# Wider value and gate projections, and a later start for two gated heads, in the second block's mixers

## The chip, the cores and the metric

One core of a Trainium2 chip runs the whole program. The metric is device time in microseconds (us): one launch from its first to its last instruction and the little that lies around it. Lower is better.

## The reference, cut to what matters

The program computes two blocks of two layers each for 512 tokens of width 1024, in fp32. The change touches only the mixer of the second block, which runs in both of its layers on 512 latent tokens and on 256 context tokens:

```python
lat, cx = project_in(h, w_in), project_in(hc, w_in)     # h @ w_in, split in ten parts
# ret: q, k, v, gate (512 columns each)   gla: q, k (256 each), v, gate (512 each), two decay inputs (16 each)
r = bidirectional_scan(retention_inputs)     # 4 heads of 128; q and k of the latent are rotated
g = bidirectional_scan(gla_inputs)           # 4 gated heads: keys of 64, values of 128, decay per key
y = concat(head_layernorm(r) * silu(ret_gate), rmsnorm(g, gla_norm_g) * silu(gla_gate))
x = x + g1 * (y @ w_out)
```

The latent scans start from the final states of the context scans. Layer 0 needs the mixer's output for the context too; layer 1 needs only its states.

## The kernel before, in words

Every large matrix product is done in three passes of fp32r matmuls (`mat3`; matmuls are recorded at L169, transposes at L186): both operands are split in a high and a low part, and hi·hi, hi·lo and lo·hi are added in PSUM. A weight block is loaded by SyncE (`wload`, L258), its high part is cast on ScalarE (ACT, L262), its low part subtracted on VectorE (DVE, L263); three blocks are in flight.

`linear` has the weights stationary and streams the tokens, 512 columns at a time for the latent. `linear_tm` has 128 tokens stationary and streams the weights; with `cn` = 256 columns two token tiles share a PSUM bank (`per` = 2), with 512 each token tile has its own bank. It opens all its banks at the start, goes through the weight blocks, and copies the banks out behind the last one, with a raised priority. In a trace a matmul of `linear_tm` reads `whi,hi` or `wlo,hi` (weights first), one of `linear` `hi,whi`.

PSUM has four banks for these products: three called `mm` and one called `bank`, which every fourth call gets. Three more are `pt` (transposes and small products), one is `po` (outputs of the heads).

`hybrid` sets up one mixer. Its projections run in a fixed order. For the latent: the decay input, the gated keys (`twice`), the gated values (`values`), the gated queries, the gated heads' gates (`gates`), the retention's keys (`heads`, L1272, rotated on GpSimd and VectorE), the retention's values, its queries, its gates. `values` and `gates` call `linear_tm` twice, with 256 columns (two heads) each. In layer 0 the context does the same but for the order of one gate; in layer 1 it has neither queries nor gates.

The heads are Python generators beside that: four gated heads (`gla`) and four retention heads (`retention`), at most two of each kind at a time (`pipe`). A generator yields a condition to wait for or a delay in planned TensorE time, so the order in which instructions are emitted is fixed when the program is built. A tile scheduler then orders each engine's queue by priority (early emission first) and by when tiles are free; on the chip every engine follows its queue in order. Most working tiles come from one pool of 36 slots (`t2`); the values of layer 1's latent have another pool (`b2`).

A gated head first turns the decay input into decays (L1417 to L1430: three activations, a scan and five VectorE operations), multiplies keys and queries (L1435 to L1443), transposes, forms scores, updates states and ends in `finish`, which multiplies by the gate (L1330), transposes, and splits the result (L420; L417 for the retention) into `y`. `y` is filled in order: gated heads 0 to 3, retention heads 0 to 3. Last comes the output product `w_out`: first the half of the gated heads, then that of the retention. In layer 0 the context's output product runs before it.

Of the kernel before, what the change touches and what calls it, by code (L numbers as in the profile page):

```python
# [13 lines left out]
AF = mybir.ActivationFunctionType  # L14
ALU = mybir.AluOpType
# [3 lines left out]
D = 1024  # L19
# [32 lines left out]
def sl(i, n=128):  # L52
    return slice(i * n, (i + 1) * n)
# [28 lines left out]
class Net:  # L82
# [1138 lines left out]
    def hybrid(self, l, h, w, st_in, st_out, outputs, rot, y):  # L1221

        nc, A = self.nc, self.A
        W = A["w_in_2"][l]
# [3 lines left out]
        V, G, F = {}, {}, {}  # L1228

        vtile = self.b2 if st_out is None and l else self.t2  # L1230

        def values(key, c0):
            for s in range(2):
                def evac(q, p):
                    t = vtile(nm="v")
                    self.evicted = nc.scalar.copy(t, p.rearrange("p i c -> p (i c)")).ins
                    for ii in range(2):
                        for hh in range(2):
                            V[key, 2 * s + hh, 2 * q + ii] = t[:, sl(ii, 256)][:, sl(hh)]

                yield from self.linear_tm(W, 0, D, c0 + 256 * s, 256, h, w, evac)

        def gates(key, c0):
            for s in range(2):
                def evac(q, p):
                    u, t = self.t2(nm="gate_in"), self.t2(nm="gate")
                    self.evicted = nc.scalar.copy(u, p.rearrange("p i c -> p (i c)")).ins
                    nc.scalar.activation(t, u, AF.Abs)
                    nc.scalar.activation(t, t, AF.Exp, scale=-1.0)
                    nc.scalar.activation(t, t, AF.Ln, bias=self.one[:, 0:1])  # L1250
                    nc.vector.scalar_tensor_tensor(t, u, 0.0, t, ALU.min, ALU.subtract)
                    nc.scalar.activation(t, t, AF.Exp)
                    nc.gpsimd.tensor_mul(t, t, u)
                    for ii in range(2):
                        for hh in range(2):
                            G[key, 2 * s + hh, 2 * q + ii] = t[:, sl(ii, 256)][:, sl(hh)]

                yield from self.linear_tm(W, 0, D, c0 + 256 * s, 256, h, w, evac)

        def narrow(nm):  # L1260

# [147 lines left out]
            yield from finish("r", hd, po.rearrange("p i c -> p (i c)"), True)  # L1409

        def gla(hd):
            yield lambda: "d" in F and ("gk", hd) in F
            p = self.pt((128, w))
            self.mat(p, self.gup[:, hd], F["d"])
            ub = self.vec("gla_gate_b_2", l * 4 + hd)
            a, b, c = (self.t2(nm=s, w=w) for s in ("ga", "gb", "gc"))
# [30 lines left out]
            p = self.pt((128, w))  # L1447
# [26 lines left out]
            for _ in range(nch // 4):  # L1474
                t = self.t2(nm="S")
# [27 lines left out]
            for cix in range(nch):  # L1503
                i, j = divmod(cix, 2)
# [3 lines left out]
        def project():  # L1508
            yield from gate_in()
            yield from twice("gk", 2304, 1.0)  # L1510
            yield from values("g", 2560)
            if outputs:
                yield from twice("gq", 2048, 0.125)
                if st_out is None:
                    yield from gates("g", 3072)
            yield from heads("rk", 512, 1.0)
            yield from values("r", 1024)
            if outputs:
                yield from heads("rq", 0, 128 ** -0.5)
                if st_out is not None:  # L1520
                    yield from gates("g", 3072)
                yield from gates("r", 1536)

        return ([self.pipe(deque(Stream(f(i)) for i in range(4)), 2) for f in (gla, retention)], project())

    def second_layer(self, l):
# [246 lines left out]
```

## Time and profile before

| what | value |
|---|---|
| median of 3 runs | 3194.77 us (3189.08 to 3195.32) |
| the profiled execution | 3192.44 us |
| its span, first to last instruction | 3190.7 us |
| TensorE busy | 3115.1 us, 98% |
| VectorE / ScalarE / GpSimd busy | 57% / 38% / 7% |
| mean granted TensorE clock | 0.991 |
| latent mixer of layer 0 / layer 1 | about 1608 to 1840 us / 2520 to 2753 us of the span |

Busy TensorE time counts from the start of a matmul to its modelled end, and neighbouring matmuls overlap; what a matmul costs in a row of its like is the distance between starts. The granted clock is a share of full speed: 1.0 is 2.4 GHz, 0.5 is 1.2 GHz.

### The profile page before, as it was taken

The page shows a single profiled execution, that of the slowest core. Times are in us where ns is not written, and L with a number is a line of the kernel's source. Part 1 is how long each engine was busy: PE and PEld are TensorE (multiplying, and loading weights), DVE is VectorE, ACT ScalarE, POOL GpSimd, SP SyncE. Part 2 cuts the span into 40 slices and gives each one's busy share as a digit, 9 for nine tenths or more (in the row PEclk, how much of TensorE's full clock was granted, in tenths as well). Part 3 has the DMA queues.
Part 4 walks back from the last instruction along what each step waited for, and adds up shares of the span by engine and source line. Part 5 has one row for each costly group of instructions (what it writes and reads, how often), then busy time and mean ns, then how long its engine had stood idle before and what let it go on. Part 6 is the DMA issues. An engine that isn't in the chain of part 4 may idle for free.

```text
span 3190.7 us, 45206 instructions
## 1 busy us (share of the span) xinstructions
PE 3115.1 (98%) x17958; PEld 2651.7 (83%) x17958; DVE 1804.6 (57%) x3261; ACT 1221.0 (38%) x2189; POOL 214.3 (7%) x263
## 2 busy tenths in 40 slices
PE   8999999999999999999998999999999998999998
PEld 8866678888997888888987998888888887978887
DVE  7865474445566664445776675333334767764444
ACT  5734342223554542223554353132222544342233
POOL 0200000000111000000121230000000012200000
PEclk9999999999999999999999999999999999999999
DMA  5357843333321223333532232121211522223332
GB/s 153 113 190 266 269 131 98 99 93 110 89 82 56 86 85 94 99 98 95 152 101 72 83 100 65 61 67 60 67 60 52 151 74 73 77 77 99 94 98 73
DMA packets 301858, 323.99 MB, mean 102 GB/s; under 512 B 18832, under 2 KB 270608, under 8 KB 301648
## 3 DMA queue, kind: packets, MB, share of 16 engines
q1 hardware_dynamic: 296656, 315.22, 32.0%
q10 hardware_dynamic: 4992, 5.90, 0.6%
q8 instruction: 141, 2.31, 0.3%
q14 instruction: 69, 0.57, 0.1%
HBM read 310.05 MB, written 2.10 MB: 98 GB/s over the span
## 4 chain that ended last, share of the span: by engine, by line
PE 92%; DVE 4%; DMA 1%; issue 1%; ACT 1%; SPq 0%; POOL 0%; ACTq 0%; DVEq 0%; POOLq 0%
PE mm L169 63%; PE bank L169 17%; PE pt L169 5%; PE po L169 3%; PE pt L186 2%; PE bank L1058 2%; DMA raw<-in_w_mem_kv 1%; DVE wlo L263 0%; PE mm L186 0%; DVE ht L1094 0%; DVE gc L1422 0%; DVE sq L381 0%; ACT whi L262 0%; DMA dup<-dup 0%; DMA ada<-in_ada_w 0%
## 5 line engine op out<-in xcount | busy, mean ns | idle before, releaser
L263 DVE TENSOR_TENSOR wlo<-raw,whi 128x1024 fp32r<-128x1024 f32 (+1 forms) x503 | 594.3, 1183 | 681.0 <-ACT whi L262 667.3
L262 ACT CAST whi<-raw 128x1024 fp32r<-128x1024 f32 (+1 forms) x503 | 505.4, 1006 | 1227.0 <-PE mm L169 821.6
L169 PE MATMUL mm<-hi,whi 128*128 128x512 f32 (+2 forms) x2276 | 723.2, 355 | 7.1 <-ACT hi L1098 2.7
L169 PE MATMUL mm<-hi,wlo 128*128 128x512 f32 (+2 forms) x1876 | 688.7, 367 | 0.8 <-DVE wlo L263 0.8
L169 PE MATMUL mm<-lo,whi 128*128 128x512 f32 (+2 forms) x1476 | 575.7, 390 | 4.5 <-DVE lo L1099 4.2
L169 PEld LDWEIGHTS mm<-hi,whi 128*128 128x128 f32 (+1 forms) x2276 | 403.5, 189 | 79.1 <-issue 6.7
L169 PEld LDWEIGHTS mm<-hi,wlo 128*128 128x128 f32 (+1 forms) x1876 | 354.6, 189 | 64.4 <-issue 7.0
L169 PE MATMUL mm<-ahi,whi 128*128 128x512 f32 (+1 forms) x1224 | 392.1, 355 | 0.0
L169 PE MATMUL mm<-ahi,wlo 128*128 128x512 f32 (+1 forms) x1032 | 377.4, 368 | 0.0
L169 PEld LDWEIGHTS mm<-lo,whi 128*128 128x128 f32 (+1 forms) x1476 | 279.3, 189 | 63.3 <-DVE lo L1099 4.7
L169 PE MATMUL mm<-alo,whi 128*128 128x512 f32 (+1 forms) x840 | 323.4, 387 | 0.0
L169 PE MATMUL mm<-whi,hi 128*128 128x256 f32 (+2 forms) x1008 | 272.2, 292 | 18.7 <-ACT qk L1272 10.3
L169 PE MATMUL mm<-wlo,hi 128*128 128x256 f32 (+2 forms) x896 | 258.8, 290 | 0.0
L169 PEld LDWEIGHTS mm<-ahi,whi 128*128 128x128 f32 x1224 | 219.2, 189 | 33.2
L169 PE MATMUL mm<-whi,lo 128*128 128x256 f32 (+2 forms) x784 | 226.1, 290 | 0.6 <-DVE lo L421 0.6
L169 PEld LDWEIGHTS mm<-ahi,wlo 128*128 128x128 f32 x1032 | 194.5, 188 | 32.4
L169 PEld LDWEIGHTS mm<-whi,hi 128*128 128x128 f32 x1008 | 188.9, 195 | 23.7 <-ACT qk L1272 11.2
L169 PEld LDWEIGHTS mm<-alo,whi 128*128 128x128 f32 x840 | 157.8, 188 | 31.3
L169 PE MATMUL bank<-hi,whi 128*128 128x512 f32 (+2 forms) x620 | 182.8, 341 | 0.8 <-DVE m L357 0.8
L169 PEld LDWEIGHTS mm<-wlo,hi 128*128 128x128 f32 x896 | 174.8, 195 | 2.8 <-issue 1.2
L169 PE MATMUL bank<-hi,wlo 128*128 128x512 f32 (+2 forms) x476 | 169.8, 357 | 0.0
L169 PEld LDWEIGHTS mm<-whi,lo 128*128 128x128 f32 x784 | 152.8, 196 | 1.3 <-DVE lo L421 0.8
(359 smaller groups left out, 4554.9 us busy)
## 6 DMA issues: line engine op xcount, KB each, us to landing
raw<-in_w_ff SPq DMA_DIRECT2D x128, 512.0 KB, 3.6
raw<-in_w_mlp SPq DMA_DIRECT2D x128, 512.0 KB, 3.6
raw<-in_w_in SPq DMA_DIRECT2D x98, 512.0 KB, 3.7
ada<-in_ada_w SPq DMA_DIRECT2D x192, 256.0 KB, 4.8
raw<-in_w_qkv SPq DMA_DIRECT2D x24, 512.0 KB, 3.5
raw<-in_w_out SPq DMA_DIRECT2D x24, 512.0 KB, 3.4
raw<-in_w_mem_kv SPq DMA_DIRECT2D x32, 256.0 KB, 3.8
raw<-in_w_mem_q SPq DMA_DIRECT2D x16, 512.0 KB, 4.0
```

Of the source, the lines that this page charges most:

```text
L169: self.last = self.nc.tensor.matmul(out, lhsT=lhsT, rhs=rhs, start=start, stop=stop, **k).ins
L186: self.nc.tensor.transpose(out, in_, self.ident)
L262: nc.scalar.copy(hi[:, v], raw[:, v])
L263: nc.vector.tensor_sub(lo[:, v], raw[:, v], f32(hi[:, v]))
L1058: m = nc.tensor.matmul(p[32 * g:32 * g + 32], lhsT=sil[:, k], rhs=w, start=(k == 0), stop=(k == KT - 1), tile_position=(0, 32 * g)).ins
```

## The change

`values` and `gates` call `linear_tm` once with 512 columns in place of twice with 256. One call for the latent so opens four banks (all there are) in place of two, for the context two in place of one. Each copied-out tile then holds one token tile of all four heads, where it held two token tiles of two heads. Weight blocks are 256 rows by 512 columns, where they were 512 by 256. And the gated heads 2 and 3 of the latent don't begin before the last of the retention's keys is in `F`.

```diff
         def values(key, c0):
-            for s in range(2):
-                def evac(q, p):
-                    t = vtile(nm="v")
-                    self.evicted = nc.scalar.copy(t, p.rearrange("p i c -> p (i c)")).ins
-                    for ii in range(2):
-                        for hh in range(2):
-                            V[key, 2 * s + hh, 2 * q + ii] = t[:, sl(ii, 256)][:, sl(hh)]
-
-                yield from self.linear_tm(W, 0, D, c0 + 256 * s, 256, h, w, evac)
+            def evac(q, p):
+                t = vtile(nm="v")
+                self.evicted = nc.scalar.copy(t, p.rearrange("p i c -> p (i c)")).ins
+                for hd in range(4):
+                    V[key, hd, q] = t[:, sl(hd)]
+
+            yield from self.linear_tm(W, 0, D, c0, 512, h, w, evac)
...
         # gates: the same change; its seven operations on each tile stay as they are
...
         def gla(hd):
-            yield lambda: "d" in F and ("gk", hd) in F
+            late = ("rk", 3) if hd > 1 and st_out is None and outputs else "d"
+            yield lambda: "d" in F and ("gk", hd) in F and late in F
```

## Rows read from the trace of the kernel before

**Rows 1.** The page: busy time by engine; the chain that ended last.
```profile
PE 3115.1 (98%) x17958; PEld 2651.7 (83%) x17958; DVE 1804.6 (57%) x3261; ACT 1221.0 (38%) x2189; POOL 214.3 (7%) x263
...
PE 92%; DVE 4%; DMA 1%; issue 1%; ACT 1%; SPq 0%; POOL 0%; ACTq 0%; DVEq 0%; POOLq 0%
```

**Rows 2.** Waits of TensorE, 1500 to 1900 us: total, times, longest.
```profile
PE mm L169 <- ACT qk L1272: 5.4, 1, 5.4
PE pt L169 <- DVE gc L1442: 2.5, 1, 2.5
PE pt L186 <- DVE gb L1435: 1.6, 1, 1.6
```

**Rows 3.** Waits of TensorE, 2550 to 2860 us.
```profile
PE pt L169 <- DVE gc L1442: 5.4, 2, 3.0
PE mm L169 <- ACT qk L1272: 4.9, 1, 4.9
```

**Rows 4.** Windows: us, busy (instructions) of each engine, PEclk, DMA share, GB/s.
```profile
1733.80:1739.20 5.40, 0.03 (x1) 0.00 (x0) 5.04 (x6) 5.27 (x9) 0.00 (x0) 0.83 0.34 102
1739.20:1744.30 5.10, 5.09 (x24) 5.10 (x25) 4.91 (x9) 1.84 (x5) 0.00 (x0) 0.51 0.35 81
...
2651.50:2655.50 4.00, 3.94 (x18) 3.94 (x19) 3.88 (x7) 1.22 (x4) 0.00 (x0) 0.50 0.50 139
...
2752.80:2797.20 44.40, 43.76 (x254) 37.63 (x252) 30.96 (x66) 14.29 (x24) 8.77 (x6) 1.00 0.19 60
```

**Rows 5.** ScalarE in order of time, layer 0: start us, us, what, idle before.
```profile
1719.02 0.57 ACT L1247 COPY gate_in<-mm 128x512 f32<-128x512 f32 x1
...
1733.03 0.69 ACT L420 ACTIVATE hi<-pt,vecs 128x512 fp32r<-128x512 f32 x1 [3.93 <-PE pt L186]
...
1734.58 0.68 ACT L1417 ACTIVATE gb<-pt,vecs 128x512 f32<-128x512 f32 x1
...
1738.58 1.06 ACT L1272 ACTIVATE qk<-mm 128x512 f32<-128x512 f32 x2
...
1780.25 1.05 ACT L1236 COPY v<-mm 128x512 f32<-128x512 f32 x2
...
1790.68 0.58 ACT L1236 COPY v<-mm 128x512 f32<-128x512 f32 x1
```

**Rows 6.** TensorE, 256 columns: first and last of 30 matmuls.
```profile
1632.25 0.28 PE L169 MATMUL bank<-whi,hi 128*128 128x256 f32 x1
...
1635.73 0.28 PE L169 MATMUL mm<-whi,lo 128*128 128x256 f32 x1
```

**Rows 7.** TensorE, 512 columns (retention's keys): first and last of 46 matmuls.
```profile
1719.90 0.39 PE L169 MATMUL mm<-hi,whi 128*128 128x512 f32 x1
...
1730.11 0.40 PE L169 MATMUL bank<-hi,whi 128*128 128x512 f32 x1
```

**Rows 8.** Tiles v and gate: copies out of PSUM; last step of gates.
```profile
L1236 ACT COPY v<-mm x16: 567/587/637, 1525.2 to 2696.1; 128x512 f32<-128x512 f32 x16
L1236 ACT COPY v<-bank x8: 568/588/601, 1531.3 to 2693.2; 128x512 f32<-128x512 f32 x8
...
L1253 POOL TENSOR_TENSOR gate<-gate,gate_in x20: 1268/1346/2329, 1594.1 to 2759.6; 128x512 f32<-128x512 f32 x20
```

**Rows 9.** Tile dup: ns min/median/max of the key product.
```profile
L1435 DVE TENSOR_TENSOR gb<-gb,dup x16: 418/688/1785, 1544.9 to 2661.5; 128x256 f32<-128x256 f32 x8, 128x512 f32<-128x512 f32 x8
```

**Rows 10.** TensorE, first matmul behind a projection: gated gates; retention's values.
```profile
1704.72 0.40 PE L169 MATMUL mm<-hi,whi 128*128 128x512 f32 x1
...
1783.36 0.40 PE L169 MATMUL mm<-hi,whi 128*128 128x512 f32 x1
```

**Rows 11.** TensorE, layer 1, behind the last gates.
```profile
2752.85 0.40 PE L169 MATMUL mm<-hi,whi 128*128 128x512 f32 x1
...
2759.28 0.60 PE L186 MATMUL pt<-ident,qk 128*128 128x128 f32 x4
...
2797.24 0.73 PE L169 MATMUL mm<-hi,whi 128*128 128x512 f32 x2 [0.68 <-ACT hi L417]
```

More of the change, by code (lines that the diff above doesn't have):

```diff
@@ L1232, in values @@
         def values(key, c0):
-            for s in range(2):
-                def evac(q, p):
-                    t = vtile(nm="v")
-                    self.evicted = nc.scalar.copy(t, p.rearrange("p i c -> p (i c)")).ins
-                    for ii in range(2):
-                        for hh in range(2):
-                            V[key, 2 * s + hh, 2 * q + ii] = t[:, sl(ii, 256)][:, sl(hh)]
-                yield from self.linear_tm(W, 0, D, c0 + 256 * s, 256, h, w, evac)
-        def gates(key, c0):
[L1244 to L1258, printed above, removed]
@@ new lines, in evac @@
+            def evac(q, p):
[4 more added lines that the diff above has]
+            yield from self.linear_tm(W, 0, D, c0, 512, h, w, evac)
+        def gates(key, c0):
+            def evac(q, p):
+                u, t = self.t2(nm="gate_in"), self.t2(nm="gate")
+                self.evicted = nc.scalar.copy(u, p.rearrange("p i c -> p (i c)")).ins
+                nc.scalar.activation(t, u, AF.Abs)
+                nc.scalar.activation(t, t, AF.Exp, scale=-1.0)
+                nc.scalar.activation(t, t, AF.Ln, bias=self.one[:, 0:1])
+                nc.vector.scalar_tensor_tensor(t, u, 0.0, t, ALU.min, ALU.subtract)
+                nc.scalar.activation(t, t, AF.Exp)
+                nc.gpsimd.tensor_mul(t, t, u)
+                for hd in range(4):
+                    G[key, hd, q] = t[:, sl(hd)]
+            yield from self.linear_tm(W, 0, D, c0, 512, h, w, evac)
```

## The prediction

> **What bounds the kernel now.** I read the page first. TensorE is busy 98% of the span, and 92% of the chain that ended last is its own work [rows 1]; so an edit pays only in what TensorE computes and in the few places where it stands. Then I asked for TensorE's waits around the two latent mixers, since the diff touches nothing else. In each mixer one wait stands out: 5.4 us in layer 0 and 4.9 us in layer 1 for L1272, the copy of the retention's keys out of PSUM [rows 2, 3]. The rest there are shorter waits for a gated head's VectorE chain: 2.5 and 1.6 us in layer 0 [rows 2], up to 3.0 us at a time in layer 1 [rows 3].
>
> What precedes the long wait stands in ScalarE's own order of time [rows 5]. It waits 3.93 us for transposes before L420 (gated head 1 ends), then runs the first activations of gated heads 2 and 3 from 1734.58, and only at 1738.58 copies the keys. TensorE has no bank for the retention's values until then. The windows show what the pause costs beyond itself [rows 4]: in the 5.10 us behind it the granted clock is 0.51, the 1.2 GHz level, after TensorE had done next to nothing for 5.4 us; in layer 1 it is 0.50 for 4.00 us.
>
> **The change part by part: the width.** A matmul of 256 columns costs (1635.73 − 1632.25) / 29 = 0.120 us from start to start [rows 6], one of 512 columns (1730.11 − 1719.90) / 45 = 0.227 us [rows 7]. The tiles copied out number 24 for values (16 + 8) and 20 for gates [rows 8], each 128x512, and their number stays. A tile takes 2 token tiles x 8 k x 3 passes = 48 narrow matmuls now, and 8 x 3 = 24 wide ones after: 48 x 0.120 − 24 x 0.227 = 0.31 us. For 44 tiles that is 14 us off TensorE, all of it on the path, as 98% busy says. Both prices are of the same fp32r matmuls at full clock, and I see no reason for another price with the operands' roles as they stand, so this term is nearly sure.
>
> A rule of the Trainium skill would make it smaller: "TensorE: Matmul & The Clock Gate", Back-to-back issue gap, gives N / 2.4 + 2.5 ns as the isolated spacing of warm matmuls (it adds that streams with weight loads differ). By that, a wide matmul saves only 2.5 ns over two narrow ones, and the 1056 pairs 2.6 us in all. The trace disagrees: 0.120 us where it gives 0.109, so I keep 14 us.
>
> Loads cost nothing more: each block is still 128x1024 per partition row, four per call, cast and subtracted as before; one feeds 24 x 0.227 = 5.4 us of TensorE for the latent where it fed 48 x 0.120 = 5.8 us. Cover is the matmuls of the block before. If it went, a block would come 0.4 us late at most. The copies and the gates' operations are the same in number and shape.
>
> **The later start.** Today heads 2 and 3 are emitted inside the keys' projection, ahead of its copies; after, behind all four of them. So their activations (1734.58 to 1738.58) no longer stand before the keys' copies [rows 5]. That takes away the 5.4 and 4.9 us and the slow stretch behind each. At 0.120 us the 24 matmuls of the first would take 2.9 of 5.10 us and the 18 of the second 2.2 of 4.00 [rows 4]: 2.2 and 1.8 us back. Together 14.3 us; the bounds are 0 (the copies stay late for another reason, a rival below) and 14.3. I take all of it.
>
> The shorter waits, 2.5 + 1.6 us in layer 0 and about as much in layer 1, come from a VectorE that is slowed: the key product L1435 takes 0.688 us as a rule and up to 1.785 [rows 9]; the slow ones, as I read the timeline, run beside GpSimd's products, the rotation's among them. Half the rotation (keys 0 and 1) would now be over before heads 2 and 3 start, half not. Bounds 0 and 8.2 us; I take half, 4.1. Heads 2 and 3 themselves start little later than now, as their activations ran at the end of the keys' projection anyway; `y` of head 3 is due only when the last gates are done, some 50 us on. No queue is passed by a DMA.
>
> **What is given back.** Three places.
>
> (a) The end of layer 1. Retention heads 0 and 1 need gates for all four token tiles. Today their gates come out of the first narrow call, half a projection before the end; after, from the last block of the wide one. In emission order heads 2 and 3 then start two blocks of the output product later, 2 x 24 x 0.227 = 10.9 us. Today their first transposes run 6.4 us behind the last gates (2752.85 to 2759.28), and TensorE waits 0.68 us for the last `y` at 2797.24 [rows 11]: no slack is left. The upper bound is therefore 10.9 us more idle time. The lower bound is 0: TensorE is full for 43.76 of these 44.40 us [rows 4], so the heads' chain queued behind the product's matmuls, and started later it would find the queue shorter. The two ends are equally near; I take 5.5. Layer 0 is covered: the context's output product runs first, 192 narrow matmuls or 23 us.
>
> (b) The retention's values in layer 0. Today the copies of their first call run at 1780.25 and the second's at 1790.68 [rows 5], 7.3 us after TensorE had left the projection at 1783.36 [rows 10]. Nobody waits, since two other banks serve meanwhile. With all four banks in one call the queries' projection has none until the first copy. Bounds 0 and 7.3 us plus some 2 us at the low clock; I take 4. Layer 1 takes its values from the other pool, and I put nothing there.
>
> (c) The gated gates, both layers. The second narrow call's copies run at 1719.02 [rows 5], 14.3 us after its matmuls (1704.72, [rows 10]). Wide, I expect two tiles to be copied at once, as the first call's are today, and two late; the keys' first half, 48 x 0.227 = 10.9 us, runs in the banks freed first, with other heads' work between. 3.4 us are uncovered at most; I take 1 in each layer, 2.
>
> For the context's calls I put nothing: two of four banks, and values half a call (5.8 us) later with the latent's projections to fill TensorE; without that cover it would be up to 5.8 us a layer.
>
> **The sum.** 14 + 14.3 + 4.1 − 5.5 − 4 − 2 = 20.9 us off the profiled execution's 3192.4 gives 3171.5. The median of the runs is 2.3 us above that execution, so 3174.
>
> **The rivals.**
>
> *Four banks at once (slower).* The copies come late wherever they come late today, now with no bank to go on with. For it: 14.3 us at the gated gates [rows 5, 10] and 7.3 us at the values. Against it: the first narrow call's gate copies are prompt. If all four gate tiles wait their 14.3 us in both layers, and (a) and (b) come at their upper ends, the loss is 28.6 + 10.9 + 9.3 = 49 us against 28 to 32 won: about +17, some 3212 us. It decides once the boundaries together cost more than 32 us. The Trainium skill warns of just this, in "Perfetto Trace Analysis", Optimizing Tensor Performance: matmul groups should rotate through banks so that the copying of one overlaps the next's matmuls. The same lines prefer larger matmuls; for this change the two pull apart.
>
> *The long wait stays under another name.* The keys' copies stand late because tiles are short, or behind the gates' activations, which now come all at once; the later start then buys nothing. For it: L420 and its 3.93 us wait stand before the keys' copies too [rows 5]. 14 − 11.5 = 2.5 us faster, 3192: no change.
>
> *Nothing is given back.* The scheduler fills all three places: 14 + 14.3 + 8.2 = 36.5 us, 3158.
>
> **How the numbers follow.** A measurement of this kernel can tell about 0.2%, 6.4 us, from no change. My forecast has 0.62, with a range of its own of 3162 to 3186; nothing given back 0.10; the wait that stays 0.14; four banks 0.14. The first two lie faster by more than 0.2%: 0.72. Same 0.14, slower 0.14. The predicted time is 3174. The range runs from 3156 (just past the third rival) to 3197 (the second, with (a) and (b) somewhat dearer), which leaves out the slower rival and little else.
>
> **What would show it.** TensorE's matmul count falls by 1056, to 16902, and wide ones behind `whi,hi` stand 0.227 us apart: the width is right. No wait of 5 us for L1272, L1272's first copies before L1417 of heads 2 and 3, a clock of 1.0 behind the keys: the later start is right. A longer wait for L417 near the end of layer 1's mixer is (a); a wait for L1236 ahead of the retention's queries (b); one for L1247 ahead of the retention's keys (c). The prediction is wrong if waits for L1236 and L1247 add up to more than 15 us, or if a new wait appears that none of these names.

## The result and the profile after

| | before | after |
|---|---|---|
| median of the runs | 3195.02 us | 3214.95 us (3213.82 to 3216.6) |
| ratio, 95% interval | | 1.0072 [1.0061, 1.0084] |
| span of the profiled execution | 3190.7 us | 3212.0 us |
| TensorE idle in it | 75.6 us | 94.0 us |
| mean granted clock | 0.991 | 0.987 |

The change costs 20 us by the medians and 23 by the ratio; the forecast was 3174, 0.6% faster. The page of the changed kernel, against [rows 1]:

```profile
PE 3118.0 (97%) x16902; PEld 2599.2 (81%) x16902; DVE 1812.5 (56%) x3261; ACT 1220.2 (38%) x2189; POOL 210.1 (7%) x263
...
PE 89%; DVE 6%; ACT 2%; DMA 1%; issue 1%; SPq 0%; POOL 0%; ACTq 0%; DVEq 0%; POOLq 0%
```

The 1056 matmuls are gone, and yet TensorE is 2.9 us *busier*: by the prediction's prices 14 us went, so what was left took some 17 us longer. To that come 18.4 us of idle time. VectorE's share of the chain rose from 4% to 6%, and TensorE's waits now name the heads. These waits, layer 0 (1500 to 1920 us; total, times, longest) and layer 1 (2560 to 2880), against [rows 2, 3]:

```profile
PE mm L169 <- ACT v L1235: 5.7, 1, 5.7
PE mm L169 <- ACT hi L417: 4.6, 1, 4.6
PE pt L169 <- DVE S L1486: 4.5, 1, 4.5
PE pt L186 <- DVE o L1326: 3.3, 1, 3.3
PE mm L169 <- ACT gate_in L1244: 1.8, 1, 1.8
```
```profile
PE pt L169 <- DVE S L1486: 5.1, 1, 5.1
PE mm L169 <- ACT gate_in L1244: 4.0, 2, 2.2
...
PE mm L169 <- ACT hi L417: 2.3, 2, 1.7
PE po L169 <- DVE o L1314: 1.8, 1, 1.8
```

The 5.4 and 4.9 us for the retention's keys (now L1268) are gone. New are the gated values (L1235), a gated head's states (L1486), and at the end of layer 0 the product with the gate (L1326) and the split into `y` (L417). Of the prediction's two signs of being wrong, one stayed away (the waits for L1235 and L1244 add up to 11.5 us, not to 15); the other, a wait that it does not name, came with L1486 and L1326. ScalarE in order of time shows the first two places (start us, us, what, idle before):

```profile
1654.72 0.61 ACT L1435 ACTIVATE ei<-gc 128x512 f32<-128x512 f32 x1
1655.24 0.57 ACT L1235 COPY v<-mm 128x512 f32<-128x512 f32 x1
...
1714.84 0.59 ACT L1316 COPY o<-po 128x512 f32<-128x512 f32 x1 [12.79 <-PE po L169]
...
1719.88 0.59 ACT L1316 COPY o<-po 128x512 f32<-128x512 f32 x1 [0.61 <-PE po L169]
...
1721.04 0.57 ACT L1244 COPY gate_in<-mm 128x512 f32<-128x512 f32 x1
...
1732.97 0.59 ACT L1268 ACTIVATE qk<-mm 128x512 f32<-128x512 f32 x1
```

The gated values' last matmul starts at 1648.7, their first copy runs at 1655.24, behind activations of the heads. The gated gates' last matmul starts at 1697.3; their first copy runs at 1721.04, behind L1316 of both heads, for which ScalarE idles 12.79 us. No bank is free until then, and the keys begin at 1721.66, not at 1704.72 [rows 10]. The windows show what TensorE did meanwhile (us, busy of PE, PEld, DVE, ACT, POOL, PEclk, DMA share, GB/s):

```profile
1697.40:1710.00 12.60, 8.92 (x76) 7.57 (x74) 8.73 (x21) 2.49 (x4) 0.00 (x0) 0.97 0.14 42
1710.00:1721.60 11.60, 7.83 (x48) 6.72 (x48) 7.28 (x22) 3.31 (x7) 0.00 (x0) 0.59 0.01 1
1721.60:1734.50 12.90, 12.84 (x51) 10.43 (x51) 7.08 (x14) 12.33 (x25) 4.53 (x4) 0.87 0.00 1
```

It ran the heads' small matmuls only, with gaps, first at a granted clock of 0.97 and then at 0.59, a mean over both levels.

The third place is the end of layer 0. The retention's split L417 runs once for each head; the rows of before (not shown ahead of the prediction) and of after:

```profile
1843.05 0.57 ACT L417 CAST hi<-pt 128x512 fp32r<-128x512 f32 x1
1844.04 0.59 ACT L417 CAST hi<-pt 128x512 fp32r<-128x512 f32 x1
1874.95 0.57 ACT L417 CAST hi<-pt 128x512 fp32r<-128x512 f32 x1
1888.31 0.59 ACT L417 CAST hi<-pt 128x512 fp32r<-128x512 f32 x1
```
```profile
1867.82 0.58 ACT L417 CAST hi<-pt 128x512 fp32r<-128x512 f32 x1
1869.08 0.57 ACT L417 CAST hi<-pt 128x512 fp32r<-128x512 f32 x1
1909.71 0.56 ACT L417 CAST hi<-pt 128x512 fp32r<-128x512 f32 x1
1919.41 0.59 ACT L417 CAST hi<-pt 128x512 fp32r<-128x512 f32 x1 [3.70 <-PE pt L186]
```

They are two pairs, and the second, 32 to 50 us behind, starts when the first is done. All four come 25 to 35 us later, and the output product, which starts at about the same time (1841), runs into them.

To follow the time through a kernel I took from the timelines when TensorE starts each stage, less the same in the kernel before (us):

| first matmul of | before | after | e1 | e5 | e9 | e15 | e16 |
|---|---|---|---|---|---|---|---|
| layer 0, latent | 1607.93 | -6.5 | +0.6 | -3.2 | +1.8 | -1.4 | -1.3 |
| gated queries | 1657.65 | -1.8 | +0.6 | -3.2 | +1.8 | +2.3 | -1.3 |
| retention's keys | 1704.72 | +16.9 | +0.5 | +11.8 | +1.8 | +6.2 | -1.3 |
| retention's queries | 1783.36 | -5.1 | -18.5 | -7.8 | -17.0 | -12.1 | -14.5 |
| output product | 1840.36 | +0.9 | -4.0 | -2.8 | -1.1 | +3.4 | -7.8 |
| end of layer 0 | 2474.46 | +15.9 | +1.9 | -1.4 | +11.6 | +8.4 | -1.5 |
| layer 1, latent | 2519.74 | +12.6 | +2.0 | -2.4 | +11.2 | +10.1 | -1.7 |
| retention's keys | 2617.51 | +29.0 | -0.7 | +13.4 | +8.6 | +11.9 | -4.4 |
| retention's queries | 2695.89 | +5.9 | -26.7 | -7.5 | -17.4 | -14.1 | -31.2 |
| output product | 2752.85 | +13.9 | -9.8 | -1.4 | +3.1 | +1.8 | -13.3 |
| end of layer 1 | 3175.09 | +21.4 | -3.8 | -2.5 | +9.9 | +8.1 | -9.4 |

"End" is the last matmul of the layer's second MLP product. Each column is one execution. Ahead of the first row nothing of this block is changed in e1, e5, e9, e15 and e16, so their -3.2 to +1.8 there are not the edit's: a column is to be read from row to row. The column of after tempts one to add up the jumps: +17 at the gated gates, +15 at the end of layer 0. The experiments show how far that goes wrong.

### The profile page after: what moved, and what is told of

Its sections match the earlier page's. It is cut to its first block, busy times and chain, and to the rows that moved or that the text cites. A ratio compares the mean times of both kernels' runs of the same rounds, so it can differ in the third digit from the quotient of the medians.

```text
span 3212.0 us, 43081 instructions
## 1 busy us (share of the span) xinstructions
PE 3118.0 (97%) x16902; PEld 2599.2 (81%) x16902; DVE 1812.5 (56%) x3261; ACT 1220.2 (38%) x2189; POOL 210.1 (7%) x263
## 4 chain that ended last, share of the span: by engine, by line
PE 89%; DVE 6%; ACT 2%; DMA 1%; issue 1%; SPq 0%; POOL 0%; ACTq 0%; DVEq 0%; POOLq 0%
PE mm L169 62%; PE bank L169 16%; PE pt L169 5%; PE po L169 3%; PE pt L186 2%; PE bank L1058 2%; DVE wlo L263 1%; DVE S L1486 1%; PE mm L186 0%; DVE ht L1094 0%; DMA raw<-in_w_mem_kv 0%; DMA ada<-in_ada_w 0%; ACT whi L262 0%; DVE gc L1419 0%; DVE sq L381 0%
## 5 line engine op out<-in xcount | busy, mean ns | idle before, releaser
L169 PE MATMUL mm<-whi,hi 128*128 128x256 f32 (+2 forms) x704 | 231.4, 339 | 8.5 <-ACT whi L262 6.3
L169 PE MATMUL mm<-wlo,hi 128*128 128x256 f32 (+3 forms) x648 | 212.8, 330 | 0.0
L169 PE MATMUL mm<-whi,lo 128*128 128x256 f32 (+3 forms) x592 | 190.5, 325 | 0.6 <-DVE lo L421 0.6
L169 PEld LDWEIGHTS mm<-alo,whi 128*128 128x128 f32 x840 | 157.8, 188 | 31.2
L169 PEld LDWEIGHTS mm<-whi,hi 128*128 128x128 f32 x704 | 134.6, 192 | 23.6 <-ACT whi L262 6.3
L169 PEld LDWEIGHTS mm<-wlo,hi 128*128 128x128 f32 x648 | 123.9, 192 | 11.4 <-issue 1.5
L169 PE MATMUL bank<-lo,whi 128*128 128x512 f32 (+2 forms) x332 | 129.8, 391 | 0.0
```

The lines of the kernel that those rows point to most:

```text
L169: self.last = self.nc.tensor.matmul(out, lhsT=lhsT, rhs=rhs, start=start, stop=stop, **k).ins
```

## The experiments

Theory A: a call that opens all four banks leaves none while its copies stand in ScalarE's queue; the later start is sound. Theory B: the later start pushes the heads into the ends. Later came theory C: the heads' chain sets the mixers' ends. All but two kernels have both forms of `values` and `gates` and a condition, so their mixers' lines stand further down (L1268 becomes L1300, L1235 becomes L1252, L1244 becomes L1260, the first activation of a gated head L1414 becomes L1446; in some runs one line more or less). The edit they share, with the condition of e1:

```diff
+        latent = st_out is None
+
+        def wide(kind, key):
+            return False
+
         def values(key, c0):
+            if not wide("v", key):
+                for s in range(2):
...
+                    yield from self.linear_tm(W, 0, D, c0 + 256 * s, 256, h, w, evac2)
+                return
```

Ratios are against the kernel before on the same chip; times in the text are (ratio - 1) x 3192 us.

**First group: e1 to e4.**

e1 keeps the later start alone (`return False`, above).

> The kernel before with the later start of gated heads 2 and 3 alone; values and gates stay 256 columns wide. Theory A (the four-bank calls cost what is lost, the later start is sound): the 5.4 and 4.9 us waits for the copy of the retention's keys go with their slow stretches, 14 to 18 us less than before, ratio 0.994 to 0.996. Theory B (the later start pushes the heads into the ends of the mixers): the same waits go, but the output products wait for the heads by 14 + 7 us as in the changed kernel; ratio 1.000 to 1.003.

e2 is all wide, without the later start:

```diff
-            late = ("rk", 3) if hd > 1 and st_out is None and outputs else "d"
-            yield lambda: "d" in F and ("gk", hd) in F and late in F
+            yield lambda: "d" in F and ("gk", hd) in F
```

> The change with its later start left out; values and gates are 512 columns wide over four banks. Theory A: the losses of the changed kernel at the gates and the ends stay and the 14 to 18 us of the later start are missing or partly missing (heads 2 and 3 then stand before the keys' copies again): ratio 1.007 to 1.012. Theory B: the ends of the mixers are free again and the 14 us of the width show: ratio 0.995 to 0.999.

e3 and e4 keep the later start and widen one kind:

```diff
-            return False
+            return kind == "g"
```

> The changed kernel with only the gates wide; values are 256 columns wide again. Theory A, with the price read from the changed kernel's trace: the gated gates still lose 17 + 13 us between their first matmul and the keys' first, the gated values' 4.5 us are gone, half the width's gain (6 us) is missing: ratio 1.003 to 1.008. Should the price lie mostly in the values (held late, so that the heads and the ends come late): below 1.000.

```diff
-            return False
+            return kind == "v"
```

> The changed kernel with only the values wide; gates are 256 columns wide again. Theory A: no wait at the gated gates, the later start's 14 us and half the width's 14 us show, the gated values lose 4.5 us in layer 0: ratio 0.993 to 0.998. If the values' late arrival is what pushes the heads into the ends of the mixers: the 14 and 7 us there stay, ratio 0.999 to 1.004.

Measured: e1 0.9989 [0.998, 0.9998]; e2 1.0138 [1.0121, 1.0155]; e3 1.0053 [1.0038, 1.0068]; e4 1.0015 [1.0005, 1.0024]. Each theory fails somewhere. B is out as the main cause: without the later start the wide kernel is slower still, by 21 us. But A's "sound" is wrong as well: alone the later start is worth 3.5 us, not 14 to 18. The keys' wait is gone from e1; in its place stand others, a gated head's (L1464) and the context's second modulation (L1115) among them (waits of e1, 1500 to 2000 us):

```profile
PE pt L186 <- DVE gb L1464: 3.6, 1, 3.6
PE mm L169 <- POOL hi L1115: 1.8, 2, 1.3
...
PE mm L169 <- ACT qk L1300: 1.4, 2, 1.3
```

Its queries begin 18.5 us earlier, its output product 4.0, and layer 0 ends 1.9 later (table): from the latent's first matmul on, e1 loses 1.3 us in layer 0 and gains 5.7 behind it. In layer 0 the heads' matmuls were only moved. Gated heads 2 and 3 begin 7 and 11 us later than before (1734.58 in [rows 5], and 1736.59; ScalarE of e1):

```profile
1741.64 0.69 ACT L1446 ACTIVATE gb<-pt,vecs 128x512 f32<-128x512 f32 x1
...
1747.28 0.69 ACT L1446 ACTIVATE gb<-pt,vecs 128x512 f32<-128x512 f32 x1
```

The retention's splits of e1 in layer 0:

```profile
1853.94 0.58 ACT L417 CAST hi<-pt 128x512 fp32r<-128x512 f32 x1 [0.44 <-PE pt L186]
...
1899.46 0.59 ACT L417 CAST hi<-pt 128x512 fp32r<-128x512 f32 x1 [3.93 <-PE pt L186]
```

They come 11 us later than before, though everything they need from the projections comes earlier. Heads that start later end later, as I read it.

**Second group: e5 to e8, the gated gates.** e5 widens one call alone; e6 gives its tiles another pool in layer 1; e7 widens all but the gated heads' two calls; e8 is e6's edit on the changed kernel.

```diff
-            return False
+            return kind == "g" and key == "g" and latent
```

> The later start, and of the projections only the gated heads' gates of the latent 512 columns wide over four banks (one call in each layer); every other value and gate 256 columns wide. Theory A (a four-bank call whose copies are held takes the retention's keys their banks): this site carries the loss of all wide gates; 2.5 us won by width, some 20 lost in the two layers: ratio 1.003 to 1.006 against 0.9989 with the later start alone. Rival (the loss is spread over all wide gates, the ends of the mixers above all): within 0.002 of 0.9989.

```diff
-            u, t = self.t2(nm="gate_in"), self.t2(nm="gate")
+            u = self.b2(nm="gate_in") if latent and l and key == "g" else self.t2(nm="gate_in")
+            t = self.t2(nm="gate")
```

> As the kernel with the gated gates alone wide, but in layer 1 the copied-out gate inputs of these four tiles come from the pool of 20 slots (b2) and not from the full one of 36 (t2); nothing else differs. Theory A1 (the copies are held because their tiles stand behind the tiles of heads 0 and 1 in the full pool): in layer 1 all four copies run within 3 us of the last gate matmul, the keys' matmuls follow without the 11 to 16 us gap, and the ratio falls by 0.003 to 0.005 against the same kernel without the pool. Theory A2 (ScalarE's order puts the heads' work first whatever the tiles): the copies stay behind the heads' copies of po and the ratio stays.

```diff
-            return False
+            return not (latent and key == "g")
```

> The later start; wide are the context's values and gates and the retention's values and gates of the latent, while the gated heads' values and gates of the latent stay 256 columns wide. 28 of 44 tiles are wide: 8.7 us off TensorE. Theory A: no site with a held copy is left, only the ends of the mixers can give back: ratio 0.995 to 0.998. Rival (late gates of the retention cost at the ends what width wins): 0.998 to 1.001.

> The changed kernel with one difference: the gated heads' gate inputs of layer 1's latent are copied into the pool of 20 slots. Theory A1: the 11 to 14 us that layer 1 loses at its gated gates go; ratio 1.002 to 1.0045 where the changed kernel has 1.0072. Theory A2: 1.006 to 1.008.

Measured: e5 1.0011 [1.0001, 1.002]; e6 1.0036 [1.0022, 1.005]; e7 1.0014 [1.0005, 1.0024]; e8 1.0077 [1.0062, 1.0092]. This is where theory A falls as the main cause. Its mechanism was right: the copies stood behind the heads because of their tiles, not because of ScalarE's order as such. ScalarE of e5, layer 1, then of e6:

```profile
2629.13 0.58 ACT L1348 COPY o<-po 128x512 f32<-128x512 f32 x1 [0.77 <-PE po L169]
2630.28 0.57 ACT L1260 COPY gate_in<-mm 128x512 f32<-128x512 f32 x1
...
2652.40 0.60 ACT L1300 ACTIVATE qk<-bank 128x512 f32<-128x512 f32 x1
```
```profile
2608.53 0.59 ACT L1261 COPY gate_in<-mm 128x512 f32<-128x512 f32 x1 [1.01 <-PE mm L169]
...
2617.72 0.59 ACT L1261 COPY gate_in<-mm 128x512 f32<-128x512 f32 x1 [2.39 <-PE mm L169]
2627.83 0.59 ACT L1349 COPY o<-po 128x512 f32<-128x512 f32 x1 [3.81 <-PE po L169]
...
2666.62 0.61 ACT L1301 ACTIVATE qk<-bank 128x512 f32<-128x512 f32 x1
```

In e6 all four copies are out at 2617.7, ahead of the heads, and the keys follow at 2617.5, 13 us sooner than in e5. Nothing is won: the keys' last copies come 14 us later than in e5, a head's product with its gate is waited for (4.6 us at L1359), and the kernel is 8 us slower by the ratios, 5 by the medians. The edit also puts four more tiles into the pool of layer 1's values, so it is not the wait's removal alone. e8, the same edit on the changed kernel, is no faster than it (1.0077 against 1.0072). In e5's layer 0 the keys start 11.8 us late, and yet from the latent's start to the layer's end it loses 1.8 us (-3.2 to -1.4), about as much as e1 (+0.6 to +1.9). In layer 0 the jump in front of the keys is not a loss: TensorE does work of the heads there that it would else do later. e7, without the gated heads' wide calls, came out just above both of its ranges.

**Third group: e9 to e12, theory C.** A retention head's last step multiplies by gates of all four token tiles. e9 widens only the retention's gates; e10 leaves only those narrow; e11 projects them before the queries, all else as in the changed kernel; e12 widens the context's calls and keeps the later start in layer 1.

```diff
-            return False
+            return kind == "g" and key == "r" and latent
```

> The later start, and of the projections only the retention's gates of the latent 512 columns wide (one call in each layer, the last before the output product). No projection but the output product follows, so no keys or queries want its banks. Theory A (held copies and missing banks are the loss): width gains 2.5 us, ratio 0.997 to 0.999. Theory C (the heads are a chain in pairs; the first pair needs all four gate tiles, whose activations now come after one another behind the call's end, and the second pair starts when the first is done): in layer 0 the splits L417 of all four retention heads come 12 to 20 us later than with the later start alone (there 1853.9, 1855.1, 1890.2 and 1899.5), and the output product waits for the last: 5 to 12 us lost in layer 0, 0 to 5 in layer 1, ratio 1.0005 to 1.004.

```diff
-            return False
+            return not (kind == "g" and key == "r" and latent)
```

> The changed kernel with the retention's gates of the latent alone 256 columns wide again. Theory C: the ends of both mixers lose little or nothing, some 14 us in layer 0 and 3 to 7 in layer 1 come back, 2.5 us of width go: ratio 1.001 to 1.0035 where the changed kernel has 1.0072. Theory A: the held copies of the gated gates and values stay, 1.006 to 1.008.

```diff
             if outputs:
+                if latent:
+                    yield from gates("r", 1536)
                 yield from heads("rq", 0, 128 ** -0.5)
                 if st_out is not None:
                     yield from gates("g", 3072)
-                yield from gates("r", 1536)
+                    yield from gates("r", 1536)
```

> The changed kernel, all values and gates wide, with the latent's retention gates projected before the retention's queries instead of behind them; the same instructions in another order. Theory C: the gate tiles are ready before the heads ask for them, so the ends lose nothing by the gates, though the heads start when the queries come, about where they do now: the splits L417 of the first pair come 8 to 15 us sooner after the last projection, ratio 1.002 to 1.005. Theory A: nothing in the banks is better, the gates' banks are now wanted by the queries: 1.007 to 1.010.

```diff
-            return False
+            return not latent
...
-            late = ("rk", 3) if hd > 1 and st_out is None and outputs else "d"
+            late = ("rk", 3) if hd > 1 and latent and l else "d"
```

> Only the context's values and gates wide (two of four banks, in both layers), the latent's all 256 columns wide, and the later start in layer 1's latent alone. From the traces so far, by stage: the context's stretch gains 5.0 us in layer 0 and 3.3 in layer 1 wherever it is wide, and layer 1's latent gains 5.8 us by the later start, layer 0's latent gains nothing by it (1.3 us lost). Theory C: these add up, 14 us less than before, ratio 0.994 to 0.997. Rival (what the context gains is taken back at the end of each mixer, which the heads' chain sets): only layer 1's 5.8 us, 0.998 to 0.9995.

Measured: e9 1.0031 [1.002, 1.0041]; e10 1.0055 [1.0041, 1.0069]; e11 1.0076 [1.0063, 1.009]; e12 0.9983 [0.9974, 0.9992]. e9 bears theory C out in the main. It costs 13 us against e1, and 4.6 us of that are a wait for its banks, by the output product of each layer (TensorE of e9):

```profile
1839.26 0.51 PE L169 MATMUL mm<-hi,whi 128*128 128x256 f32 x2 [2.38 <-ACT gate_in L1260]
...
2755.98 0.50 PE L169 MATMUL mm<-hi,whi 128*128 128x512 f32 x1 [2.20 <-ACT gate_in L1260]
```

Its splits, 12 and 16 us behind e1's:

```profile
1866.12 0.57 ACT L417 CAST hi<-pt 128x512 fp32r<-128x512 f32 x1
...
1915.17 0.59 ACT L417 CAST hi<-pt 128x512 fp32r<-128x512 f32 x1 [3.69 <-PE pt L186]
```

e10 gained only 5 us on the changed kernel, which the intervals hardly tell from none and which is less than C expected: its splits still run from 1863.43 to 1910.59, so with late values the chain is late anyway, as I read it. e11 fell into theory A's range: with gates early but the queries last, the splits run from 1881.20 to 1922.65. That what comes last sets the heads' start, whichever it is, would fit; it is not shown. e12 lies in its rival's range; in its trace the context's 5.0 us of layer 0 are taken back (latent begins 3.1 us early, layer 0 ends 5.5 late).

**Fourth group: e13 to e16.** e13 reads no gates in the changed kernel, e14 none in the kernel before; e15 and e16 widen one values call each.

```diff
-                nc.vector.scalar_tensor_tensor(o3[:, i], o3[:, i], r[:, i:i + 1], G[key, hd, i], ALU.mult, ALU.mult)
+                nc.vector.scalar_tensor_tensor(o3[:, i], o3[:, i], r[:, i:i + 1], self.one, ALU.mult, ALU.mult)
```

> The changed kernel in which the heads multiply by a resident tile of ones where they multiplied by their gates; the gates are still projected and computed, in the same place, but no head waits for one. (Left out: the product with the gates.) Theory C1 (what the ends of the mixers lose is the wait for gates that now come all at the call's end): the splits L417 of layer 0 come 10 us sooner or more, the output products' waits for L417 and L1326 go, 15 to 21 us less than the changed kernel: ratio 1.0005 to 1.003. Theory C2 (the heads' chain is late before its gates: values, states and the order of the pairs): ratio 1.005 to 1.0075.

> The same replacement in the kernel before, as the control. (Left out: the product with the gates.) Theory C1 and C2 alike: no wait of TensorE in the kernel before stands behind a gate, so 0.997 to 1.000; were it much faster, the gates would have bound the kernel before as well.

```diff
-            return False
+            return kind == "v" and key == "g" and latent
```

> The later start, and of the projections only the gated heads' values of the latent 512 columns wide (one call in each layer). Theory of sites (each wide call has a price of its own, here the 5.7 us wait for L1235 and the slow stretch behind it in layer 0): 2.5 us won, 6 to 9 lost in layer 0, nothing in layer 1: ratio 1.000 to 1.002. If what the wide values cost comes from the retention's values: 0.997 to 0.9995.

```diff
-            return False
+            return kind == "v" and key == "r" and latent
```

> The later start, and of the projections only the retention's values of the latent 512 columns wide (one call in each layer). Theory of sites: the changed kernel's trace shows no wait at this call, so the 2.5 us of its width are won: 0.997 to 0.999. If the retention heads' pairs are pushed by their values coming all at the call's end: the end of layer 0 loses, 0.9995 to 1.002.

Measured: e13 1.0025 [1.0015, 1.0035]; e14 0.9999 [0.999, 1.0009]; e15 1.0032 [1.0021, 1.0042]; e16 0.9971 [0.9959, 0.9983]. Without the wait for gates, in gated and retention heads alike, the changed kernel is 15 us faster, and the kernel before does not care. From the output product to the end of layer 0, e13 loses 3.8 us on the kernel before (+0.9 to +4.6), where the changed kernel loses 15.0 (table). Splits of e13:

```profile
1856.42 0.57 ACT L417 CAST hi<-pt 128x512 fp32r<-128x512 f32 x1
...
1907.76 0.59 ACT L417 CAST hi<-pt 128x512 fp32r<-128x512 f32 x1 [4.37 <-PE pt L186]
```

So C1 holds, with a limit: the first is 11 us sooner than in the changed kernel, yet 13 behind before, of which e1 has 11 as well. And up to 3.4 of the 15 us may not be the gates': in e13 the order of the queues differs a little, and the wait for L1235 is gone. e15 puts 13.7 us on the gated values, above its range; ScalarE and TensorE of e15:

```profile
1658.30 0.63 ACT L1463 ACTIVATE gb<-gb 128x512 f32<-128x512 f32 x1 [1.01 <-DVE gc L1459]
...
1659.36 0.56 ACT L1252 COPY v<-mm 128x512 f32<-128x512 f32 x1
```
```profile
1659.98 0.80 PE L169 MATMUL mm<-hi,whi 128*128 128x512 f32 x1 [6.00 <-ACT v L1252]
```

The queries wait 6.00 us for that copy, and 3.7 us are lost on e1 by then; the rest comes behind it, and the heads' splits are 7 to 8 us later (1861.82 to 1906.88). e16 is faster than both kernels. Against e1 it gains 5.7 us, of which the width is 2.5; the rest is hardly clear of the intervals. Its heads 2 and 3 begin as early as before, though their condition is that of e1 (ScalarE of e16; why is not shown):

```profile
1734.40 0.70 ACT L1446 ACTIVATE gb<-pt,vecs 128x512 f32<-128x512 f32 x1
...
1736.43 0.67 ACT L1446 ACTIVATE gb<-pt,vecs 128x512 f32<-128x512 f32 x1
```

**Last group: e17 and e18**, the context's calls added to e16, and e16 without the later start (edit as in e2).

```diff
-            return False
+            return not latent or kind == "v" and key == "r"
```

> The later start, with the latent's retention values and all of the context's values and gates 512 columns wide; the latent's other three calls 256. If the price of a wide call is that of its own site and the context's are free: 3 to 8 us less than with the retention's values alone (0.9971): ratio 0.9945 to 0.996. If what the context's stretch gains is taken back by the heads behind it, as the run with the context alone wide suggests: 0.9965 to 0.9985.

> Only the latent's retention values 512 columns wide, and gated heads 2 and 3 start as in the kernel before. If width and later start add up (3.6 us by the later start, 5.7 by this call): ratio 0.998 to 0.999. If the call's four banks need the later start (its copies then stand behind the activations of heads 2 and 3, and its banks behind the keys' copies): 1.000 to 1.006.

Measured: e17 0.9975 [0.9965, 0.9985]; e18 1.0023 [1.0013, 1.0034]. The context adds nothing to e16 that the intervals could show. The later start is what makes the wide call pay: it is worth 17 us with it and 3.5 without. In e18 heads 2 and 3 stand before the keys' second pair of copies again (ScalarE, then TensorE of e18):

```profile
1735.80 1.07 ACT L1300 ACTIVATE qk<-mm 128x512 f32<-128x512 f32 x2
1739.39 0.63 ACT L1462 ACTIVATE gb<-gb 128x512 f32<-128x512 f32 x1 [2.53 <-DVE gc L1458]
...
1747.33 0.58 ACT L1300 ACTIVATE qk<-mm 128x512 f32<-128x512 f32 x1
```
```profile
1736.43 0.80 PE L169 MATMUL mm<-whi,hi 128*128 128x512 f32 x1 [5.38 <-ACT qk L1300]
...
1747.96 0.50 PE L169 MATMUL mm<-whi,hi 128*128 128x512 f32 x1 [1.82 <-ACT qk L1300]
```

The 5.38 us for the first pair stand in the kernel before as well [rows 2]. A call that needs four banks waits a second time, 1.82 us, for the second pair, where one that needs two would not. The retention's queries begin 7.5 us later than before, counted from the latent's first matmul (1605.16 to 1788.09); how much of that the second wait brings about is not shown. The lowest ratio is e16's, 0.9971, with the later start and one wide call of the eight that the diff has in layer 0; the intervals of e17, e12 and e1 overlap with its own.

## Why the prediction was wrong

Each latent call's price is now known by itself: its run against e1 (all with the later start). Each is good to some 4 us by the intervals. With nothing for the context they nearly add up: -3.5 (later start) - 5.7 + 7.0 + 13.7 + 13.4 = +24.9 us for the changed kernel, where 23.0 were measured; for e3, e4 and e7 the sums are 16.9, 4.5 and 4.2, measured 16.9, 4.8 and 4.5. For e10 the sum is 11.5, and 17.6 were measured, so the calls may not be independent. A latent call has 8 tiles in both layers, so its width is worth 8 x 0.31 = 2.5 us, the context's 12 tiles 3.7.

| step of the prediction | predicted, us | measured, us |
|---|---|---|
| later start, with the short VectorE waits | -18.4 | -3.5 (e1) |
| gated values: nothing given back | -2.5 + 0 | +13.7 (e15) |
| (c) gated gates | -2.5 + 2 | +7.0 (e5) |
| (a) retention's gates; layer 0 covered | -2.5 + 5.5 | +13.4 (e9) |
| (b) retention's values | -2.5 + 4 | -5.7 (e16) |
| context | -3.7 | +1.3, not clear of zero (e17 against e16) |

- **The step that failed** is the first: "all of it on the path, as 98% busy says". The width's mechanism was right (16902 matmuls, the wide ones 0.227 us apart from 1635.83 to 1641.50 as forecast), as was the later start's (no wait for L1268, copies at 1732.97, a granted clock of 1.00 from 1746.60 to 1760.00). But TensorE's busy share did not make its work the only bound. Beside it runs a chain of heads in pairs, nearly as long as the mixer (its last split before is at 1888.31, the output product ends at 1921), and time taken off TensorE came back as waits for that chain. Taking "all of" the 14.3 us and half of the short waits, without asking what is late next, is 15 of the 44 us between forecast and result. The gated values, which have no term at all, are 16 more, the retention's gates 10.
- **"Heads 2 and 3 themselves start little later than now"** is where the later start failed: alone it starts them 7 and 11 us later, and the retention's splits follow 11 us later (e1). Some 9 us were forecast in each layer; layer 0 lost 1.3, and 5.7 were gained behind it.
- **"Layer 0 is covered"** failed. Cover of 23 us was counted, but the four splits were never set against the product that reads them: in the kernel before the last of them runs at 1888.31, when a product that ends at 1921 still has room; the later start took 11 us of it (e1), the wide gates another 16 (e9). In the table e9 loses 8.5 us more than e1 in layer 0 and 4.0 in layer 1; for layer 1 the forecast, 5.5 less 1.25 of width, was about right.
- **Gated values: no term.** Of the latent's late values the prediction prices the retention's alone. A wait for L1235 was named as a sign only ahead of the retention's queries. It came one call earlier, ahead of the gated ones.
- **(c)** named the right wait, and its trace looked worse than forecast (17 us in front of the keys). Measured alone it is 7 us, 9.5 given back with the width. In e6 the visible wait went and the kernel got no faster; what the call costs, in layer 1, stays open.
- **(b)** did not come: e16 gives nothing back. The retention heads' splits in e16 come 4 to 7 us sooner than in e1.
- **The rival "four banks at once"** gave 3212 and was right in sign and size, but not in its sum: it had (b) at 9.3 and the gates at 28.6, and lacked the gated values and the end of layer 0. The Trainium skill's advice that it leaned on ("Perfetto Trace Analysis", Optimizing Tensor Performance: let matmul groups rotate through the banks) gives the right sign here, but the runs bear out its reason only in part: in e9, which cost 13 us, the waits for the wide call's banks are 4.6, and a call on all four banks paid (e16).

Open stays what the gated gates cost in layer 1, and why the context's gain in its own stretch is lost behind it; e12 and e17 show only that it is. Not run is a call of 512 columns for two token tiles at a time, which would tell the price of the width from that of four banks.

## What to carry to other kernels

A bound by busy time is a bound only if the chain beside it has slack: before pricing a saving on the busiest engine, list when each product of the slow chain lands and when it is read, at the end of the stage above all. Merging two calls into one delivers the first half's results at the second half's time; what that costs is set by who starts on the first half. A wait in a trace shows where time is standing, not where it is lost: take the wait away alone, as e6 tried, before believing its length.

## What the runs showed of the hardware

The clock turned waits into more than their length. After the gated gates of the changed kernel TensorE had 48 small matmuls in 11.60 us, and the granted clock of that window was 0.59, a mix of the two levels, where it had been 0.97 just before; the next 12.90 us, 99% busy, were granted 0.87. The same stands in layer 1 (0.59 in the 11.50 us from 2635.00). Over the whole span the mean clock fell from 0.991 to 0.987, by which 0.004 x 3200 = 13 of the 17 us that the remaining matmuls took longer would be the clock's, an estimate.
